# Seven-product steps that add up in place, and one ring for the weight tiles, in a hybrid decoder layer

## The chip, the cores and the metric

The kernel runs on one core of one Trainium2 chip. The metric is the device time of one execution in microseconds; lower is better. Runs of the same kernel agree within about 0.1%.

## What is computed

One inference step of one decoder layer, in float32, on 2048 prompt tokens (one sequence) and 32 sample tokens (eight sequences of four). Cut to what matters here:

```
h = x + mixer(rmsnorm(x))                          # gated linear attention beside a spatial-gating MLP
q = rmsnorm(h) @ wq_x                              # cross attention over 256 memory tokens, 4 heads
p = softmax(q @ mem_k.T / 16)
h = h + (p @ mem_v) @ wo_x
g = rmsnorm(h) @ w_gate                            # 1024 -> 2816
c = conv_b + sum(conv_w[j] * shift(g, j))          # causal depthwise convolution of width 3
h = h + (gelu(c) * (rmsnorm(h) @ w_up)) @ w_down   # 2816 -> 1024
y = rmsnorm(h)
```

It also returns the recurrent and convolution states and the memory keys and values.

## The kernel before

The prompt is worked in four blocks of 512 tokens (`SB`, s = 0 to 3). The 32 sample tokens ride with block 1 in the mixer and with block 2 in the ConvFFN, so block 2's ConvFFN has 544 tokens. Between, during block 1's ConvFFN, the sample tokens' cross attention runs in small steps (`sample_steps`).

*Precision.* Every large product is made of three float32r matmuls (`mm3`): each operand is split into a high part (an ACT copy) and a low part (a DVE subtraction, `split`), and high x high, high x low and low x high are added in PSUM. A float32 weight tile that came by DMA is called raw (tag `wraw`, five buffers); its two parts are `whi` and `wlo` (five buffers each). Weights that were split once can be stored in DRAM and fetched in two parts without a split (`wready`).

*Seven products for eight.* In blocks 1 to 3 the gate and up projections (`gate7`, `upp7`), and in all blocks the scores of the cross attention (`score`), use Strassen's scheme in Winograd's form: the weight matrix and the activations are cut 2 by 2, and seven products of half size take the place of eight. Three products use quarters of the weight matrix as they are (A11, A12, A22, called `PLAIN`), four use sums of quarters (S1 to S4, `SUMS`). `seven_tokens` makes the activations' sums. `seven_make` makes the weights' sums in block 0, from the raw tiles that block 0 needs anyway, and stores them in DRAM: for the gate split in two parts, for up unsplit. A seven-product step (`seven_step`) has seven products of 12 matmuls, each into a PSUM bank or half of one (`acc`, four banks), and combines them with ACT and DVE in a tile q of the raw pool: q0 takes a copy of A11, q3 = S2 + q0, then q1, q2 and q3 get S1 and S3, q0 gets A12, q1 and q2 get S4 and A22. The gate of the first pair in a block (j = 0) runs in an "early" form: all seven banks are open at once, so that most of its work can start before the last activations are there. In block 2 a half has 272 columns, and two halves don't fit a bank; in blocks 1 and 3 it has 256, and two share a bank (`joint`).

*Order.* A list of `Step`s is written out, with side work woven in (`weave`), and `run` goes through it: ahead of each step it issues the loads of later ones, up to `AHEAD` = 5 units further, where a unit is a pair of split tiles (a `seven_tile` counts half). All loads and stores are issued by SP, in one queue. The framework then orders the instructions of each engine when the program is built, by a timeline of its own, from these priorities and from what each instruction waits for, so an instruction may stand ahead of one that comes earlier in the list. On the chip each engine goes through its own order.

*Other tiles.* `U` (49 buffers) and `T_` (6) are general tiles of 544 columns: T holds the gate rows g, the convolved rows c and other short-lived ones.

Of the kernel before, what the change touches and what calls it, by code (L numbers as in the profile page):

```python
# [9 lines left out]
F32 = mybir.dt.float32  # L10
F32R = mybir.dt.float32r
# [18 lines left out]
AHEAD = 5  # L30
NU, NT, NRAW, NW = 49, 6, 5, 5
# [6 lines left out]
def hymba_step_kernel(  # L38
# [16 lines left out]
    wp = ctx.enter_context(tc.tile_pool(name="wp", bufs=NW))  # L55
    npool = ctx.enter_context(tc.tile_pool(name="npool", bufs=8))
# [7 lines left out]
    def T_(name, dt=F32):  # L64
        return tp_.tile([128, TM], dt, tag="T", name=name)
# [25 lines left out]
    def mm3(ps, wh, wl, xh, xl, first, last):  # L91
        pe.matmul(ps, wh, xh, start=first, stop=False)  # L92
        pe.matmul(ps, wh, xl, start=False, stop=False)  # L93
        pe.matmul(ps, wl, xh, start=False, stop=last)  # L94

    def wraw(name):
        return wp.tile([128, 2 * TM], F32, tag="wraw", name=f"r_{name}", bufs=NRAW)

    def wload(w, k0, nk, m0, mw, name):
        raw = wraw(name)  # L100
        r3 = raw[:, :nk * mw].rearrange("p (k m) -> p k m", k=nk)
        nc.sync.dma_start(r3, w[k0 * 128:(k0 + nk) * 128, m0:m0 + mw].rearrange("(k p) m -> p k m", p=128))
        return r3

    def wsplit(raw, name, lo_eng=None):
        sh = list(raw.shape)
        hi = wp.tile(sh, F32R, tag="whi", name=f"h_{name}")
        lo = wp.tile(sh, F32R, tag="wlo", name=f"l_{name}")
        split(hi, lo, raw, lo_eng)
        return hi, lo  # L110

    def wunit(*spec):
        return wsplit(wload(*spec), spec[-1])

    def wraw_unit(*spec):
        return lambda: wload(*spec)

    def wready(src, name):

        def load():  # L120
            out = []
            for x, tag in enumerate(("whi", "wlo")):
                t = wp.tile(list(src.shape[0:1]) + list(src.shape[2:]), F32R, tag=tag, name=f"{tag}_{name}")
# [3 lines left out]
        return load  # L127

    def wkeep(dst, *spec):

        def load():
            out = wunit(*spec)
# [3 lines left out]
        return load  # L136
# [3 lines left out]
    PLAIN, SUMS = ("A11", "A12", "A22"), ("S1", "S3", "S2", "S4")  # L140
    w7n = [0]

    def seven_tile(src, name):

        def load():
            w7n[0] += 1
            t = wp.tile([128, 2, 4, 128], F32R, tag=("whi", "wlo")[w7n[0] % 2], name=name)
            nc.sync.dma_start(t.bitcast(F32), src)
            return t
        load.cost = 0.5  # L150
        return load

    def seven_make(raw, hi, lo, plain, sums, u, name):
# [4 lines left out]
        s13, s24 = U(f"s13{name}"), U(f"s24{name}")  # L158
        h3 = lambda t, i: t[:, i * 256:(i + 1) * 256].rearrange("p (k m) -> p k m", k=2)
        dve.tensor_tensor(h3(s13, 0), a21, a22, ALU.add)  # L160
        dve.tensor_tensor(h3(s13, 1), a11, a21, ALU.subtract)
        dve.tensor_tensor(h3(s24, 0), h3(s13, 0), a11, ALU.subtract)
        dve.tensor_tensor(h3(s24, 1), a12, h3(s24, 0), ALU.subtract)
        ks = slice(2 * u, 2 * u + 2)
        for x, t in enumerate((hi, lo)):
# [4 lines left out]
        for i, t in enumerate((s13, s24)):  # L170
            d = sums[:, 2 * i:2 * i + 2]
            v = lambda t: t.rearrange("p (s k m) -> p s k m", s=2, k=2)
# [33 lines left out]
    def seven_sums(src, name):  # L206

        def load():
            raw = wraw(name)
            nc.sync.dma_start(raw[:, :1024], src.rearrange("p s k m -> p (s k m)"))  # L210
            return wsplit(raw[:, :1024].rearrange("p (k m) -> p k m", k=8), name)
        return load

    def seven_step(plain, sums, get_xs, H, use, name, early=False, then=None):


        seq = ("A11", "S1", "A12", "S2", "S3", "S4", "A22") if early else ("A11", "S2", "S1", "S3", "A12", "S4", "A22")
        joint = 2 * H <= 512 and not early

        units, at = [], {}  # L220
        for nm in seq:
            if nm in PLAIN or len(sums.shape) == 5:
                at[nm] = len(units), None
                units.append(seven_tile(plain[:, PLAIN.index(nm)] if nm in PLAIN else sums[:, SUMS.index(nm)],
                                        f"{name}{nm}"))
            elif nm not in at:
                i = SUMS.index(nm) // 2
                for j in range(2):
                    at[SUMS[2 * i + j]] = len(units), j
                units.append(seven_sums(sums[:, 2 * i:2 * i + 2], f"{name}{nm}"))  # L230

        def fn(*ws):
            def half(nm, x, k):
                u, j = at[nm]
                return ws[u][:, x, k] if j is None else ws[u][x][:, 4 * j + k]

            xs = get_xs()
            last = len(xs) - 1
            q = wraw(f"q_{name}")
            q0, q1, q2, q3 = (q[:, i * H:(i + 1) * H] for i in range(4))  # L240
            ps = {}

            def prod(nm, k0, k1):
                if nm not in ps:
                    mate = {"S3": "S1", "A22": "S4"}.get(nm)
                    if joint and mate:
                        ps[nm] = ps[mate][0], 1
                    else:
                        ps[nm] = (mps if early and len(ps) > 3 else acc)(f"a_{name}{nm}"), 0
                bank, i = ps[nm]  # L250
                for k in range(k0, k1):
                    mm3(bank[:, i * H:(i + 1) * H], half(nm, 0, k), half(nm, 1, k), *xs[k][nm], k == 0, k == last)

            def got(nm):
                return ps[nm][0][:, ps[nm][1] * H:(ps[nm][1] + 1) * H]

            def c11():
                dve.tensor_tensor(q0, got("A12"), q0, ALU.add)

            if early:  # L260
                for nm in seq:
                    prod(nm, 0, last)
            for nm in seq:
                prod(nm, last if early else 0, last + 1)
                if then and nm == "S1":
                    then()
                if nm == "A11":
                    act.activation(q0, got(nm), AF.Copy)
                elif nm == "S2":
# [1573 lines left out]
```

## Time and profile before

| what | value |
|---|---|
| median of three runs | 2832.87 us (2832.57 to 2835.03) |
| the profiled execution | 2837.18 us, of which 2835.5 are the span of the trace |
| TensorE (PE) busy | 2797.1 us, 99% |
| VectorE (DVE) busy | 1894.6 us, 67% |
| ScalarE (ACT) busy | 1106.0 us, 39% |
| GpSimd (POOL) busy | 569.5 us, 20% |
| read from and written to HBM | 507.69 and 127.41 MB |

The ConvFFN of block 0 lies at about 400 to 750 us of the span, block 1's at 1100 to 1500, block 2's at 1820 to 2150, block 3's at 2480 to 2800. In a table by stage, each row begins with the stretch in microseconds; for each engine stands its busy time and the number of its instructions, then the clock that TensorE was granted (1.00 is full), the mean busy share of the sixteen DMA engines, and GB/s. In a time line, a row is start, duration, engine, line, operation and tiles, and in brackets the idle time just before it and what ended that. In a list of groups, the last part is the idle time ahead of the group's instructions and what ended it. PEld is the load of the stationary operand, which overlaps PE.

### The profile page before, as it was taken

The numbers are of one execution on the slowest core, as the hardware profiler recorded it, in microseconds if no ns is written. First come the engines' busy times: TensorE is split into PE (matmuls) and PEld (weight loads), VectorE is DVE, ScalarE is ACT, GpSimd is POOL, SyncE is SP. The second block draws the span as 40 slices with busy tenths as digits, with TensorE's granted clock in tenths as the row PEclk, the third lists the DMA queues.
The fourth block names the chain that finished last, engine by engine and source line by source line (L and its number), as shares of the span: only waits on it lengthen the run. The fifth ranks groups of instructions, "written<-read, shape, count | busy, mean of one in ns | idle before, by whom it ended". The sixth has DMA issues, their size and how long they took to land.

```text
span 2835.5 us, 47052 instructions
## 1 busy us (share of the span) xinstructions
PE 2797.1 (99%) x17894; PEld 2477.9 (87%) x17894; DVE 1894.6 (67%) x3266; ACT 1106.0 (39%) x1950; POOL 569.5 (20%) x638
## 2 busy tenths in 40 slices
PE   8999999999999999999999999999999999999998
PEld 8888888888887898898888889899999888899997
DVE  6578778777657786655555778666666687665555
ACT  5645544333363354223124445422223544431222
POOL 2002213111111221322210121222221022132222
PEclk9999999999999999999999999999999999999999
DMA  9756589999932245888995216577776323677774
GB/s 297 250 182 219 180 267 341 336 343 329 337 112 68 85 154 195 314 288 291 331 324 190 82 60 208 194 252 258 258 269 207 112 69 128 206 260 273 272 281 177
DMA packets 369687, 638.21 MB, mean 225 GB/s; under 512 B 27370, under 2 KB 238412, under 8 KB 369462
## 3 DMA queue, kind: packets, MB, share of 16 engines
q1 hardware_dynamic: 369462, 635.20, 65.7%
q8 instruction: 142, 2.33, 0.3%
q14 instruction: 83, 0.68, 0.1%
HBM read 507.69 MB, written 127.41 MB: 224 GB/s over the span
## 4 chain that ended last, share of the span: by engine, by line
PE 63%; DVE 3%; ACT 1%; issue 0%; POOL 0%; DMA 0%; POOLq 0%; DVEq 0%; ACTq 0%
PE d L94 4%; PE d L92 4%; PE d L93 4%; PE a_wx L94 2%; PE a_wx L93 2%; PE a_wx L92 2%; PE a_wo L92 1%; PE s L1046 1%; PE a_wo L93 1%; PE a_wo L94 1%; PE a_wu L92 1%; PE a_wu L93 1%; PE t_wr L92 1%; PE t_wr L93 1%; PE a_wu L94 1%; PE t_wr L94 1%
## 5 line engine op out<-in xcount | busy, mean ns | idle before, releaser
L92 PE MATMUL d<-acth,whi_wd 128*128 128x272 f32 (+1 forms) x688 | 235.4, 342 | 0.0
L1692 DVE TENSOR_TENSOR h<-d,h 128x512 f32<-128x512 f32 (+1 forms) x232 | 133.7, 582 | 149.4 <-PE d L94 149.2
L94 PE MATMUL d<-acth,wlo_wd 128*128 128x272 f32 (+1 forms) x688 | 233.4, 340 | 0.0
L93 PE MATMUL d<-actl,whi_wd 128*128 128x272 f32 (+1 forms) x688 | 233.3, 339 | 0.0
L1589 POOL TENSOR_TENSOR c<-c,bc_f 128x512 f32<-128x512 f32 (+1 forms) x88 | 137.0, 1562 | 140.4 <-ACT c L1588 139.7
L1579 ACT ACTIVATE c<-g,colsb 128x512 f32<-128x512 f32 x88 | 71.7, 815 | 189.7 <-DVE g L1542 141.7
L94 PEld LDWEIGHTS d<-acth,wlo_wd 128*128 128x128 f32 x688 | 129.5, 188 | 15.5 <-issue 1.2
L93 PEld LDWEIGHTS d<-actl,whi_wd 128*128 128x128 f32 x688 | 129.5, 188 | 13.5 <-issue 0.4
L92 PEld LDWEIGHTS d<-acth,whi_wd 128*128 128x128 f32 x688 | 129.6, 188 | 13.1
L1611 POOL TENSOR_TENSOR c<-r_q_wup,c 128x512 f32<-128x512 f32 (+1 forms) x33 | 63.3, 1918 | 329.4 <-DVE r_q_wup L288 209.6
L92 PE MATMUL a_wo<-ch,h_wo 128*128 128x512 f32 (+1 forms) x320 | 114.3, 369 | 2.0 <-ACT r L876 1.3
L1576 POOL COPY carry<-g 128x2 f32<-128x2 f32 x88 | 29.5, 335 | 420.8 <-DVE g L1542 418.8
L93 PE MATMUL a_wo<-cl,h_wo 128*128 128x512 f32 (+1 forms) x320 | 113.8, 358 | 0.0
L94 PE MATMUL a_wo<-ch,l_wo 128*128 128x512 f32 (+1 forms) x320 | 112.9, 356 | 0.0
L1580 DVE SCALAR_TENSOR_TENSOR c<-g,colsb,c 128x512 f32<-128x512 f32 x88 | 84.9, 965 | 28.3 <-ACT c L1579 27.8
L94 PE MATMUL a_wx<-pTh,wlo_wx 128*128 128x512 f32 x256 | 101.3, 396 | 0.0
L93 PE MATMUL a_wx<-pTl,whi_wx 128*128 128x512 f32 x256 | 100.6, 393 | 0.0
L92 PE MATMUL a_wx<-pTh,whi_wx 128*128 128x512 f32 x256 | 100.2, 394 | 0.0
L84 ACT ACTIVATE acth<-c 128x512 fp32r<-128x512 f32 (+1 forms) x88 | 55.9, 637 | 109.6 <-DVE c L1611 78.0
L1588 ACT ACTIVATE c<-c 128x512 f32<-128x512 f32 (+1 forms) x88 | 56.1, 637 | 94.5 <-DVE c L1581 82.6
L1581 DVE SCALAR_TENSOR_TENSOR c<-g,colsb,c 128x512 f32<-128x512 f32 x88 | 90.6, 1029 | 1.1
L85 DVE TENSOR_TENSOR actl<-c,acth 128x512 fp32r<-128x512 f32 (+1 forms) x88 | 63.1, 720 | 26.6 <-ACT acth L84 25.6
(3753 smaller groups left out, 9741.8 us busy)
## 6 DMA issues: line engine op xcount, KB each, us to landing
whi_wd<-wd SPq DMA_DIRECT2D x66, 512.0 KB, 7.7
wlo_wd<-wd SPq DMA_DIRECT2D x66, 512.0 KB, 7.3
r_wo<-in_w_out_dram SPq DMA_DIRECT2D x32, 512.0 KB, 3.4
wlo_wx<-vod SPq DMA_DIRECT2D x32, 512.0 KB, 4.2
whi_wx<-vod SPq DMA_DIRECT2D x32, 512.0 KB, 5.0
r_wg<-in_w_gate_dram SPq DMA_DIRECT2D x22, 512.0 KB, 7.6
r_wup<-in_w_up_dram SPq DMA_DIRECT2D x22, 512.0 KB, 5.3
r_wd<-in_w_down_dram SPq DMA_DIRECT2D x22, 512.0 KB, 4.5
```

What stands on the lines that cost most here:

```text
L84: act.activation(hi, src, AF.Copy)
L85: (lo_eng or dve).tensor_tensor(lo, src, hi.bitcast(F32), ALU.subtract)
L92: pe.matmul(ps, wh, xh, start=first, stop=False)
L93: pe.matmul(ps, wh, xl, start=False, stop=False)
L94: pe.matmul(ps, wl, xh, start=False, stop=last)
L1579: act.activation(c[:, :SB], g[:, 2:SB + 2], AF.Identity, bias=cb, scale=w2)
L1580: dve.scalar_tensor_tensor(c[:, :SB], g[:, 1:SB + 1], w1, c[:, :SB], ALU.mult, ALU.add)
L1581: dve.scalar_tensor_tensor(c[:, :SB], g[:, 0:SB], w0, c[:, :SB], ALU.mult, ALU.add)
L1588: act.activation(c[:, :T], c[:, :T], AF.Gelu_apprx_tanh)
L1589: pool.tensor_tensor(c[:, :T], c[:, :T], B.fbc[:, :T], ALU.mult)
L1611: (dve, pool)[i].tensor_tensor(c[:, :T], q[i], c[:, :T], ALU.mult)
L1692: dve.tensor_tensor(B.h[m + mm][:, cs], ps[:, :cw], B.h[m + mm][:, cs], ALU.add)
```

## The change

- *One ring.* `whi` and `wlo` become one tag `w` of ten tiles of 1024 columns; `wraw` becomes `raw`, three tiles of 1024 columns. `run` counts, in place of `AHEAD`, which tiles of the ring and which raw tiles (those that a step itself reads) are still to be used, and issues a load when there is room. A seven-product step is seven steps now, one for each product, so a weight tile is given back with its product.
- *In place.* Except in the early gate, the products add up in PSUM along chains: A11, S2, S3 in x; A12 in z; S1, S4 in y; A22 in w. ACT copies x after A11 (to q0) and after S2 (to q1), w after A22 (to q2), y after S1 (to q3); after S3 one DVE operation adds x to q2 and q3, and after S4 one adds z and y to q0 and q1. Where two halves fit a bank, x and w share one, and z and y share one, with y continuing on what z holds. The scores go the same way, with a bank for each chain. The order of the products changes to A11, A12, S2, S1, A22, S3, S4 (scores: A11, S1, A12, S2, A22, S3, S4).
- *Gate sums unsplit.* They are stored like up's: one tile of raw sums for two products, split when it is fetched. The sums are paired S1 with S4 and S2 with S3.
- *Tiles.* q is no raw tile any more: for the gate it is the tile g itself, for up two T tiles. T goes from 6 buffers of 544 columns to 8 of 552, U from 49 to 51.

The diff, cut to its core:

```diff
-AHEAD = 5
-NU, NT, NRAW, NW = 49, 6, 5, 5
+TW = 552
+NU, NT, NW, NR = 51, 8, 10, 3
...
+    def W(name):
+        return wp.tile([128, 1024], F32R, tag="w", name=name)
+    def unit_of(load, ring=2, raws=0, held=False):
+        load.ring, load.raws, load.held, load.until = ring, raws, held, None
+        return load
+    def raw_tile(name):
+        return rp.tile([128, 1024], F32, tag="raw", name=f"w_{name}")
...
-    PLAIN, SUMS = ("A11", "A12", "A22"), ("S1", "S3", "S2", "S4")
+    PLAIN, SUMS = ("A11", "A12", "A22"), ("S1", "S4", "S2", "S3")
+    CHAIN = {"A11": "x", "S2": "x", "S3": "x", "S1": "y", "S4": "y", "A12": "z", "A22": "w"}
+    COPIED = {"A11": 0, "S2": 1, "A22": 2, "S1": 3}
...
     # seven_make
-            if len(sums.shape) == 4:
-                nc.sync.dma_start(d[:, :, ks], v(t[:, :512]))
-                continue
-            sh, sl = U(f"sh{i}{name}", F32R), U(f"sl{i}{name}", F32R)
-            split(sh[:, :512], sl[:, :512], t[:, :512])
-            for x, o in enumerate((sh, sl)):
-                nc.sync.dma_start(d[:, :, x, ks], v(o[:, :512].bitcast(F32)))
+            nc.sync.dma_start(sums[:, 2 * i:2 * i + 2, ks], t[:, :512].rearrange("p (s k m) -> p s k m", s=2, k=2))
...
     # seven_step, one product
+        def part(nm, *ws):
+            i = CHAIN[nm]
+            if nm in loads:
+                hold(nm, *ws)
+            if nm == "A11":
+                st.q, st.at = outs(), {}
+            if i not in st.at:
+                if joint:
+                    t = acc(f"a_{name}{i}")
+                    for n, o in enumerate("xw" if i in "xw" else "zy"):
+                        st.at[o] = t[:, n * H:(n + 1) * H]
+                    if i in "zy":
+                        st.zy = t[:, 0:2 * H]
+                else:
+                    st.at[i] = acc(f"a_{name}{i}")[:, :H]
+            fresh = nm in ("A11", "A12") or not joint and nm in ("S1", "A22")
+            for k in range(last + 1):
+                mm(st.at[i], nm, k, fresh and k == 0, k == last)
...
+            if nm in COPIED:
+                act.activation(quarters(q)[COPIED[nm]], st.at[i], AF.Copy)
+            elif nm == "A12" and not joint:
+                q0 = quarters(q)[0]
+                dve.tensor_tensor(q0, st.at["z"], q0, ALU.add)
+            elif nm == "S3":
+                q23 = q[1].rearrange("p (s t) -> p s t", s=2)
+                dve.tensor_tensor(q23, st.at["x"].unsqueeze(1).broadcast_to([128, 2, H]), q23, ALU.add)
+            elif nm == "S4":
+                if joint:
+                    dve.tensor_tensor(q[0], st.zy, q[0], ALU.add)
...
+        parts = {nm: Step(lambda *ws, nm=nm: part(nm, *ws), [unit(nm)] if nm in loads else []) for nm in seq}
+        for nm in SUMS[::2]:
+            parts[nm].units[0].until = parts[SUMS[SUMS.index(nm) + 1]]
+        return Step(None, parts=list(parts.values()))
...
     # run
-            need += sum(cost(u) for u in st.units)
-            while at < len(queue) and made < need + AHEAD:
+            for live in (ring, raws):
+                while live and live[0][1] < i:
+                    live.pop(0)
+            while at < len(queue):
                 j, u = queue[at]
...
+                if not (room(ring, "ring", u.ring, NW) and room(raws, "raws", u.raws, NR)):
+                    break
...
     # score
-        SEQ = ("A11", "S1", "A12", "S2", "S3", "S4", "A22")
+        SEQ = ("A11", "S1", "A12", "S2", "A22", "S3", "S4")
...
+                fresh = nm in ("A11", "S1", "A12", "A22")
+                if fresh:
+                    B.ps[CHAIN[nm]] = acc(f"sc{s}{i}{nm}")
+                ps = B.ps[CHAIN[nm]]
...
+                if nm in COPIED:
+                    o = COPIED[nm]
+                    q[o] = T_(f"p{s}{i}{o}")
+                    act.activation(q[o][:, :512], ps, AF.Copy)
+                for o in {"A12": (0,), "S3": (3, 2), "S4": (1,)}.get(nm, ()):
+                    dve.tensor_tensor(q[o][:, :512], ps, q[o][:, :512], ALU.add)
+                    soften(i, o)
```

More of the change, by code (lines that the diff above doesn't have):

```diff
@@ L485, in run, with room @@
     def run(steps):
+        steps = [p for st in steps for p in st.parts]
+        index = {st: i for i, st in enumerate(steps)}
         queue = [(i, u) for i, st in enumerate(steps) for u in st.units]
-        cost = lambda u: getattr(u, "cost", 1)
         ready = {}
-        made = need = 0
+        ring, raws = [], []
+        made = {"ring": 0, "raws": 0}
         at = 0
+        def room(live, kind, n, size):
+            return not live or made[kind] + n - live[0][0] <= size
         for i, st in enumerate(steps):
@@ L742, in load @@
                 return raw, *wsplit(raw, f"{name}{j}")
-            return load
-        return [Step(lambda wu, j=j: fn(j, wu), [unit(j)]) for j in range(4)]
+            return unit_of(load, 2, 1, sample)
+        out = [Step(lambda wu, j=j: fn(j, wu), [unit(j)]) for j in range(4)]
+        for j in (0, 2) if sample else ():
+            out[j].units[0].until = out[j + 1]
+        return out
     def norm_in_steps(B):
```

290 lines of the change are left out of this document (125 added, 165 removed).

## The prediction

> **What bounds the kernel now.** I read the page's busy times first, then the busy time by stage, then what each engine waited for, and last the time line around the places that the change touches.
>
> ```profile
> span 2835.5 us, 47052 instructions
> PE 2797.1 (99%) x17894; PEld 2477.9 (87%) x17894; DVE 1894.6 (67%) x3266; ACT 1106.0 (39%) x1950; POOL 569.5 (20%) x638
> HBM read 507.69 MB, written 127.41 MB: 224 GB/s over the span
> ```
>
> ```profile
> core 0: us, PE busy (x) PEld busy (x) DVE busy (x) ACT busy (x) POOL busy (x), PEclk, DMA share, GB/s
> 0.00:50.00 50.00, 41.21 (x301) 38.90 (x302) 31.48 (x62) 30.27 (x58) 14.85 (x57) 1.00 0.93 297
> 400.00:750.00 350.00, 350.00 (x1525) 285.13 (x1525) 269.54 (x430) 142.40 (x188) 66.88 (x72) 1.00 1.04 332
> 1010.00:1038.00 28.00, 24.24 (x185) 23.06 (x183) 27.92 (x55) 19.68 (x35) 11.56 (x8) 0.99 0.28 84
> 1038.00:1050.00 12.00, 11.88 (x76) 11.56 (x76) 5.78 (x12) 2.90 (x5) 2.66 (x3) 0.74 0.30 101
> 1050.00:1500.00 450.00, 450.00 (x3322) 400.45 (x3321) 256.40 (x401) 133.69 (x229) 106.20 (x121) 1.00 0.82 294
> 1850.00:2150.00 300.00, 300.00 (x2397) 300.00 (x2397) 192.01 (x347) 73.26 (x117) 78.81 (x119) 1.00 0.74 262
> 2500.00:2800.00 300.00, 300.00 (x2138) 281.21 (x2137) 175.51 (x247) 71.08 (x105) 80.11 (x82) 1.00 0.78 276
> ```
>
> TensorE bounds it. In the four ConvFFN stages (the 400, 1050, 1850 and 2500 rows) PE is busy for every microsecond while DVE, ACT and the DMA engines have room, except in block 0, where the DMA share is 1.04 and PE is full all the same. PE loses time in few places: 8.8 us in the first 50, and 3.8 us in 1010 to 1038, where DVE is busy for 27.92 of 28 us and the clock then drops to 0.74 for 12 us (another 3.1 us). Over the whole span PE is idle for 2835.5 - 2797.1 = 38 us, so no edit that leaves the matmuls alone can win much more than 1.5%.
>
> **The change, part by part.** The matmuls stay: 66 seven-product steps of 84 and 56 score products of 24, with the same shapes. Thus the sum is made of PE's waits alone.
>
> *Sums in place.* Before, each product had a bank or half of one, and DVE combined them; now A11, S2 and S3 add up in x, S1 and S4 in y, and ACT copies A11, S2, A22 and S1 out in between.
>
> ```profile
> L275 DVE TENSOR_TENSOR r_q_wg<-a_wg13S,r_q_wg x1: 692/692/692, 1231.3 to 1231.3; 128x512 f32<-128x512 f32 x1
> L281 DVE TENSOR_TENSOR r_q_wg<-a_wg13S,r_q_wg x1: 424/424/424, 1232.0 to 1232.0; 128x256 f32<-128x256 f32 x1
> L84 ACT ACTIVATE sh0wg<-s13wg 128x512 fp32r<-128x512 f32 x22 | 13.9, 633 | 46.9 <-DVE s13wg L161 45.5 <-DMA wd<-l_wd 1.3
> L85 DVE TENSOR_TENSOR sl0wg<-s13wg,sh0wg 128x512 fp32r<-128x512 f32 x22 | 15.0, 682 | 0.0
> L84 ACT ACTIVATE h_wup<-r_wup 128x1024 fp32r<-128x1024 f32 x22 | 23.3, 1057 | 26.9 <-PE d L93 15.4 <-issue 3.6 <-PE a_wg L93 3.4
> L85 DVE TENSOR_TENSOR l_wup<-r_wup,h_wup 128x1024 fp32r<-128x1024 f32 x22 | 28.1, 1279 | 6.1 <-ACT h_wup L84 6.0
> ```
>
> DVE: a step with both halves in one bank (42 of them: blocks 1 and 3 without the early gate) goes from 3 x 0.42 + 2 x 0.69 = 2.6 us to 2 x 0.69 = 1.4; the 21 of block 2 from seven operations to three, about -1.4 each; the eight score groups lose three of 0.69. Together -53 - 29 - 17 = -99 us. *Gate sums unsplit:* 66 splits are added where the gates run, 66 x 1.28 = +84 us on DVE and 66 x 1.06 = +70 on ACT; 44 half-size ones go from block 0, -30 and -28. DVE ends about 45 us lower, ACT with 189 copies of 0.38 (row below) and 24 in the scores of about 0.6 some 128 us higher, at 44% of the span. Both lie beside a full PE: DVE has 125 us free in the 300 of the last stage, ACT 229, so neither total reaches the end: 0. The sums' DMAs halve for the gates: 33 steps x 1 MB less read, 11 MB less written, and SP issues 66 loads and 44 stores fewer. Block 0 is relieved, but PE was full there: 0. If that cover went, its bound is the DMA share of 1.04, and it falls.
>
> *What is new on the path* is that PE now waits for ACT. S2 may not start before A11 is copied, with one product (A12) between; A22 and S3 sit likewise behind copies. Before, the A11 copy (L268) had nobody waiting, so its lateness is ACT's own queue, and it can be read off:
>
> ```profile
> 2614.82 0.28 PE L94 MATMUL a_wup34A<-w1wx,wup34A 128*128 128x256 f32 x1
> 2614.94 0.28 PE L92 MATMUL a_wup34S<-wuhwx,h_wup34S 128*128 128x256 f32 x1
> 2615.14 0.38 ACT L268 ACTIVATE r_q_wup<-a_wup34A 128x256 f32<-128x256 f32 x1 [11.60 <-PE a_wup34A L94]
> ```
>
> ```profile
> L94 PE MATMUL a_wg11A<-w1wx,wg11A x4: 280/282/284, 1149.8 to 1150.9; 128*128 128x256 f32 x4
> L94 PE MATMUL a_wg19A<-w1wx,wg19A x4: 274/280/282, 1439.1 to 1440.1; 128*128 128x256 f32 x4
> L94 PE MATMUL a_wg110A<-w1wx,wg110A x4: 275/280/283, 1462.4 to 1463.5; 128*128 128x256 f32 x4
> ```
>
> ```profile
> 1154.69 0.63 ACT L84 ACTIVATE acth<-c 128x512 fp32r<-128x512 f32 x1 [0.51 <-POOL c L1611]
> 1155.22 0.36 ACT L268 ACTIVATE r_q_wg<-a_wg11A 128x256 f32<-128x256 f32 x1
> 1440.11 0.63 ACT L760 ACTIVATE junk<-x 128x512 bf16<-128x512 f32 x1 [11.71 <-DMA x<-in_x_prompt_dram]
> 1444.19 0.36 ACT L268 ACTIVATE r_q_wg<-a_wg19A 128x256 f32<-128x256 f32 x1
> 1467.46 0.38 ACT L268 ACTIVATE r_q_wg<-a_wg110A 128x256 f32<-128x256 f32 x1 [1.97 <-PE sop L1406]
> 1840.37 0.38 ACT L268 ACTIVATE r_q_wg<-a_wg21A 128x272 f32<-128x272 f32 x1
> 2503.26 0.36 ACT L268 ACTIVATE r_q_wg<-a_wg31A 128x256 f32<-128x256 f32 x1
> ```
>
> The usual case is the first: the matmul that starts last at 2614.82 has its copy done at 2615.52, 0.70 us later. The next products follow at 0.12 us a matmul, so with A12's twelve between, S2 could start 0.12 + 12 x 0.12 = 1.55 us after: covered. Of the 63 copies of steps that will chain, the rows show three in block 1 that came late, because ACT, in order, stood behind something else: an activation split behind POOL, a square that waited 11.71 us for the DMA of x, a sample matmul. Their lateness over 1.55 us: 1155.58 - 1150.9 - 1.55 = 3.1; 1444.55 - 1440.1 - 1.55 = 2.9; 1467.84 - 1463.5 - 1.55 = 2.8. Two more, the second gates of blocks 2 and 3 (1840.37, 2503.26), end about 2.1 us after their last matmul: 0.5 each. Sum 9.8 us. Bounds: 0, if the order of the engines, which is planned anew, puts other matmuls there; and twice 9.8 if S2's copies, with the same cover, meet as much. I take one draw, since a stop of 3 us at A11 has let the blocking instruction pass before S2 is done, and leave out the case that hangs on the DMA of x, as the sums that crowd its queue are halved: **+7 us**.
>
> *Order of the scores.* S3 moves behind A22, so of the first five units fetched ahead only S1 and S2 need a split.
>
> ```profile
> L85 DVE TENSOR_TENSOR l_qk10S<-r_qk10S,h_qk10S 128x1024 fp32r<-128x1024 f32 x3 | 3.7, 1218 | 0.0
> 1034.85 1.21 DVE L85 TENSOR_TENSOR l_qk10S<-r_qk10S,h_qk10S 128x1024 fp32r<-128x1024 f32 x1
> ```
>
> The third split, at 1034.85, lies inside the stretch where DVE holds PE up; moved on, it gives back its 1.2 us. Bounds: 0, and all of 3.8 + 3.1 = 6.9 with the clock. I take the nearest row: **-1.2 us**.
>
> *One ring of ten, three raw tiles.* Ten split tiles were there before (two tags of five); released product by product they hold the same number in flight. Raw tiles fall from five to three.
>
> ```profile
> 3.40 5.19 SPq L102 DMA_DIRECT2D r_wk<-in_wk_x_dram  x5
> 18.13 0.38 SPq L102 DMA_DIRECT2D r_wk<-in_wk_x_dram  x1
> 25.08 1.06 ACT L84 ACTIVATE h_wk<-r_wk 128x1024 fp32r<-128x1024 f32 x1 [4.35 <-DMA r_wk<-in_wk_x_dram]
> r_wd<-in_w_down_dram SPq DMA_DIRECT2D x21, 512.0 KB, 4.5
> r_wup<-in_w_up_dram SPq DMA_DIRECT2D x20, 512.0 KB, 5.3
> r_wg<-in_w_gate_dram SPq DMA_DIRECT2D x19, 512.0 KB, 8.2
> ```
>
> In block 0 a raw tile lives for a transfer (4.5 to 8.2 us) plus the split (1.06 + 1.28), 7 to 11 us; three of them deliver a unit each 2.3 to 3.5 us, while PE takes 24 x 0.23 = 5.5 us for one (350 us / 1525 matmuls): covered. SP's order changes with it: what stands behind a load that waits for a raw tile are the stores of the split weights, and their cover is the four units held ahead. At the start there is no cover: five loads go out at once, the sixth at 18.13, and ACT then waits 4.35 us for it. With three, the fourth and fifth must wait for the first split (DVE ends it about 12.2 us), 7 us later than now, but the sixth no longer stands behind the loads of x. Bounds: -2.7 and +4; I take **+1.5**.
>
> *T 6 to 8, U 49 to 51.* The q tiles leave the raw pool for T (two per step), so T's room is as before; no wait of the rows above names a U tile: 0.
>
> Sum: 7 - 1.2 + 1.5 = +7.3 us. The profiled execution took 2837.18 us for its span of 2835.5, 1.7 around it; the median of the runs shown is 2832.87, 4.3 under. On the median: 2832.87 + 7.3 = **2840**.
>
> **The rivals.**
> *A: it stays hidden.* 58 of the 63 copies were in time, and the order is planned with the new waits in it, so PE may be given `d`, next-step or sample matmuls to run meanwhile. For: PE full in all three stages. Against: ACT's late ones come from waits of up to 11.7 us. Then only the small terms are left: 2833.
>
> *B: faster.* DVE loses the third split and PE's pause at 1028 to 1038 closes. It decides once DVE is about 4 us ahead in that stretch, for then the clock does not drop either: -6.9, with the start's 1.5 won as lost, 2825. Against: nothing else of DVE's 27.92 us there goes away.
>
> *C: halves of a bank wait for each other.* In 42 steps x and w lie in one bank, and S3 stands right behind A22. If a matmul into one half is held until the copy of the other is done, each such step stops for 0.70 - 0.12 = 0.58 us: 42 x 0.58 = 24 us, 2857. For: the order written out has nothing in between. Against: S4 writes the other bank and could be put there.
> The Trainium skill, "PSUM — Partial Sum Buffer", section "PSUM bank collisions raise a hardware error", says that engines must be kept apart by bank and quadrant, not by address; by it the copy of A22 and S3 cannot overlap, and the sum would be C's unless other matmuls fill in. The trace of before has no matmul into a bank with a reader at work in its other half, so it does not show this.
>
> **How the numbers follow.** Forecast 0.38, A 0.30, B 0.20, C 0.12. About 0.2% (5.7 us) is what a measurement here can tell from no change; a tenth of the forecast's chance falls below it. Slower 0.34 + 0.12 = 0.46, same 0.30 + 0.04 = 0.34, faster 0.20. The range reaches from B's 2825 to C with some of the forecast's term, 2861; the forecast alone holds 2835 to 2852 (0 to 20 for the late copies).
>
> **What would show it.** Chain waits: PE idle in front of a_wg or a_wup with an ACT copy as releaser, most of it in block 1 (1100 to 1500), PE no longer 450 of 450. C: the same pause of about 0.6 us in every step of block 3. Scores: two splits instead of three in the stretch before the scores of block 1, and PE's loss there under 3.8. Start: PE under 41.2 of the first 50. The forecast is wrong if PE stays full in the ConvFFN stages, or if a whole stage starves for weights because three raw tiles are too few, which no term above prices.

## The result, and the profile after

The changed kernel took 2880.33 us (median of six runs, 2875.52 to 2883.46), the kernel before 2834.95 beside it (2832.57 to 2839.88): a ratio of 1.0158, with an interval from 1.0144 to 1.0172. It is some 45 us slower, outside the range of the prediction (2825 to 2861 around 2840). The profiled execution took 2877.25 us, 40 more than that of before. Runs of the kernel before, beside all the kernels below, lie between 2830.6 and 2841.5 us but for one of 9728, so they agree within 0.4%, not the 0.1% given at the top.

The page after, its head and its line of HBM traffic:

```profile
span 2875.5 us, 46693 instructions
PE 2807.7 (98%) x17894; PEld 2482.3 (86%) x17894; DVE 1835.4 (64%) x3054; ACT 1216.2 (42%) x2185; POOL 562.7 (20%) x638
HBM read 473.09 MB, written 115.87 MB: 205 GB/s over the span
```

The volumes moved much as forecast: DVE by -59 (forecast -45), ACT by +110 (forecast +128), HBM by -34.6 and -11.5 MB. The time went the other way, because PE is idle for 2875.5 - 2807.7 = 68 us instead of 38, and it is busy 10.6 us longer for the same matmuls. The granted clock, 0.995 of full over the span before and 0.992 after, makes some 8 to 9 us of that by an estimate from the two; what makes the rest isn't shown. The busy times by stage (the start, then the four ConvFFN stages), and after them the two stages of the kernel before that lost most, over the same work:

```profile
0.00:50.00 50.00, 41.35 (x301) 38.61 (x301) 30.72 (x61) 29.17 (x59) 13.73 (x57) 1.00 0.88 274
424.00:774.00 350.00, 350.00 (x1540) 285.27 (x1539) 242.68 (x391) 120.16 (x156) 53.42 (x69) 1.00 0.99 318
1136.00:1547.00 411.00, 400.96 (x2979) 354.55 (x2978) 226.11 (x291) 150.06 (x259) 98.99 (x116) 0.99 0.75 261
1838.00:2209.00 371.00, 370.58 (x2962) 369.95 (x2961) 227.35 (x391) 147.17 (x262) 102.86 (x140) 1.00 0.62 220
2503.00:2865.00 362.00, 352.68 (x2442) 326.37 (x2442) 193.52 (x252) 130.43 (x220) 78.12 (x93) 0.99 0.62 214
```

```profile
1126.00:1524.00 398.00, 398.00 (x2978) 352.77 (x2977) 225.76 (x333) 110.71 (x176) 99.11 (x116) 1.00 0.83 297
2479.00:2825.00 346.00, 346.00 (x2442) 322.76 (x2441) 201.02 (x295) 87.17 (x137) 86.85 (x93) 1.00 0.71 254
```

Blocks 1 and 3, where two sums of a gate or up step share a bank, have the same 2979 (one more than before, at the edge of the stretch) and 2442 matmuls in 411 and 362 us that took 398 and 346. Block 2, with a bank for each sum, is full. Some of what PE waited for in the kernel after: a wait in block 1's mixer (t_wr1q), and the longest ones ahead of gate and up products, of which the kernel before had none over 0.2 us (total, times, longest):

```profile
PE t_wr1q L745 <- DMA w_wr<-in_w_in_dram: 4.0, 1, 4.0
PE a_wup15x L93 <- ACT q L292: 2.6, 1, 2.6
PE a_wg32x L93 <- DMA wg32A<-w7g: 2.5, 1, 2.5
PE a_wg16x L93 <- DMA wg16A<-w7g: 2.3, 1, 2.3
PE a_wg12x L93 <- DVE c L1605: 2.2, 1, 2.2
PE a_wg38x L93 <- DMA wg38A<-w7g: 2.1, 1, 2.1
PE a_wg310x L93 <- DVE nct L1780: 1.6, 1, 1.6
PE a_wg18x L93 <- DMA wg18A<-w7g: 1.4, 1, 1.4
PE a_wg34x L93 <- DMA wg34A<-w7g: 1.2, 1, 1.2
```

Only one of these ends on a copy by ACT. The others of the ConvFFN stages stand before A11 of an even gate, the first of a group, and most end on the load of its weight tile. How block 3 gets there shows in PE's order, taken from the time line as products (start in us; a product that is split stands once, where it begins):

```
before  2500.15 wg31: A11 S2 S1 S3 A12 S4 A22   2510.05 wup31: A11 S2 S1 S3 A12 S4 A22   2519.95 wg32: A11
after   2526.04 wup30 S4, S3 | 2528.89 wg31 S2, S4 | 2531.72 wup31 A11, A12 | 2533.70 wg31 A22
        2536.07 wup31 S1 | 2537.48 wg31 S3 | pause | 2541.65 wg32 A11, A12, S1 | 2547.53 wup31 S2
```

The list has A22, S3, S4 at the end of a step; the order that was planned has the next step's A11, A12 and S1 in between, since A22 goes into the half bank beside x and must wait for the copy of S2, and S3 for the copy of A22. Two steps thus want weight tiles at once: up to 14 by count (three single tiles and two pairs for each), and the ring has ten. The load of wg32's tile goes out late, behind SP's other waits. The first row below shows why: ACT's split of wup31's sums had to wait until 2528.73 for a tile of the ring that a product of wup30 still read. The raw tile of these sums came free only after the split, at 2532, and SP stood for it with the loads of wg32 behind it (ACT, SP, then PE, from the time line):

```profile
2528.73 2.01 ACT L85 ACTIVATE h_wup31S<-w_wup31S 128x1024 fp32r<-128x1024 f32 x2 [1.29 <-PE a_wup30x L95]
```

```profile
2528.60 0.32 SPq L154 DMA_DIRECT2D wup31A<-w7u  x1
2532.03 0.32 SPq L206 DMA_DIRECT2D w_wg32S<-s7g  x1
2532.41 0.42 SPq L154 DMA_DIRECT2D wup31A<-w7u  x1
2533.77 0.32 SPq L206 DMA_DIRECT2D w_wup32S<-s7u  x1
2534.18 1.44 SPq L154 DMA_DIRECT2D wg32A<-w7g  x2
```

```profile
2538.90 0.27 PE L1778 MATMUL ncp<-ident,carry 128*2 128x128 f32 x1
2541.65 0.36 PE L93 MATMUL a_wg32x<-w1wx,wg32A 128*128 128x256 f32 x1 [2.48 <-DMA wg32A<-w7g]
```

### The profile page after: what moved, and what is told of

The parts are those of the page before. It is cut to its first block, busy times and chain, and to the rows that moved or that the text cites. A ratio compares the mean times of both kernels' runs of the same rounds, so it can differ in the third digit from the quotient of the medians.

```text
span 2875.5 us, 46693 instructions
## 1 busy us (share of the span) xinstructions
PE 2807.7 (98%) x17894; PEld 2482.3 (86%) x17894; DVE 1835.4 (64%) x3054; ACT 1216.2 (42%) x2185; POOL 562.7 (20%) x638
## 4 chain that ended last, share of the span: by engine, by line
PE 83%; DMA 6%; DVE 5%; ACT 3%; issue 2%; POOL 1%; SPq 0%; POOLq 0%; ACTq 0%; DVEq 0%
PE d L95 6%; PE d L93 6%; PE d L94 6%; PE a_wx L95 2%; PE a_wx L94 2%; PE a_wx L93 2%; PE s L1082 2%; PE a_wg L95 1%; PE a_wup L95 1%; PE a_wup L93 1%; PE a_wg L93 1%; PE a_wg L94 1%; PE a_wup L94 1%; PE a_wu L95 1%; PE a_wu L93 1%
## 5 line engine op out<-in xcount | busy, mean ns | idle before, releaser
L93 PE MATMUL d<-acth,h_wd 128*128 128x512 f32 (+1 forms) x864 | 305.0, 354 | 0.9 <-DMA h_wd<-wd 0.9
L95 PE MATMUL d<-acth,l_wd 128*128 128x512 f32 (+1 forms) x864 | 302.6, 351 | 1.3 <-DMA l_wd<-wd 1.3
L94 PE MATMUL d<-actl,h_wd 128*128 128x512 f32 (+1 forms) x864 | 303.2, 351 | 0.0
L95 PEld LDWEIGHTS d<-acth,l_wd 128*128 128x128 f32 x864 | 162.4, 188 | 24.1 <-DMA l_wd<-wd 2.1
L93 PEld LDWEIGHTS d<-acth,h_wd 128*128 128x128 f32 x864 | 162.4, 188 | 22.7 <-PE sop L1429 1.4
L94 PEld LDWEIGHTS d<-actl,h_wd 128*128 128x128 f32 x864 | 162.7, 188 | 20.5 <-issue 0.6
L1636 POOL TENSOR_TENSOR c<-q,c 128x512 f32<-128x512 f32 (+1 forms) x33 | 48.5, 1470 | 412.7 <-DVE q L298 289.5
L95 PE MATMUL a_wx<-pTh,l_wx 128*128 128x512 f32 x256 | 100.7, 394 | 0.0
L94 PE MATMUL a_wx<-pTl,h_wx 128*128 128x512 f32 x256 | 100.3, 393 | 0.0
L93 PE MATMUL a_wx<-pTh,h_wx 128*128 128x512 f32 x256 | 98.8, 394 | 0.0
L1605 DVE SCALAR_TENSOR_TENSOR c<-g,colsb,c 128x512 f32<-128x512 f32 x88 | 69.6, 795 | 16.3 <-ACT c L1604 16.3
```

Of the source, the lines that this page charges most:

```text
L93: pe.matmul(ps, wh, xh, start=first, stop=False, skip_group_check=again)
L94: pe.matmul(ps, wh, xl, start=False, stop=False, skip_group_check=again)
L95: pe.matmul(ps, wl, xh, start=False, stop=last, skip_group_check=again)
L1605: dve.scalar_tensor_tensor(c[:, :SB], g[:, 1:SB + 1], w1, c[:, :SB], ALU.mult, ALU.add)
```

## The experiments

Beside the kernel after, fourteen kernels were run. For each the table has the median, its ratio to the kernel before with the interval, and, from the profiled executions, how much longer than before each stretch took (us; from the first matmul of one tile to that of the next). A stretch "to FFN n" is block n's mixer and scores; the first begins at the program's start. Each stretch comes from one execution; in the last row, where nothing changed in the median, stretches still differ by up to 2.4 us.

| kernel | median us | ratio | to FFN 0 | FFN 0 | to FFN 1 | FFN 1 | to FFN 2 | FFN 2 | to FFN 3 | FFN 3 |
|---|---|---|---|---|---|---|---|---|---|---|
| after | 2880.3 | 1.0158 [1.0144, 1.0172] | +7.4 | -0.1 | +2.3 | +13.1 | +0.8 | +0.3 | +0.2 | +16.0 |
| four banks | 2867.5 | 1.0116 [1.0097, 1.0135] | +9.3 | -0.1 | +4.8 | +12.0 | +0.9 | +1.2 | -0.5 | +3.1 |
| four banks, 49 U | 2862.6 | 1.0092 [1.0073, 1.0112] | +7.9 | -2.7 | +5.6 | +6.8 | +3.4 | +0.7 | -0.6 | +3.8 |
| four raw tiles | 2859.7 | 1.0078 [1.0062, 1.0095] | -1.3 | -0.9 | -3.2 | +10.0 | +3.7 | +1.5 | -0.7 | +13.0 |
| four banks, four raw | 2842.5 | 1.0026 [1.0017, 1.0036] | +2.1 | -0.9 | -1.8 | +3.1 | +1.8 | +0.1 | +0.3 | +1.1 |
| ring of eleven | 2873.9 | 1.0134 [1.0120, 1.0148] | +12.6 | +1.6 | +1.9 | +10.2 | -0.1 | +1.4 | -1.4 | +6.9 |
| control 48 U, 7 T | 2905.8 | 1.0247 [1.0232, 1.0262] | +16.2 | +3.8 | +7.7 | +16.3 | +2.2 | +1.9 | +1.4 | +14.4 |
| ring of twelve, 48, 7 | 2885.5 | 1.0177 [1.0162, 1.0192] | +20.3 | +3.2 | +5.4 | +9.3 | +2.2 | +4.6 | +1.6 | +4.1 |
| five raw, 48, 7 | 2874.1 | 1.0135 [1.0120, 1.0150] | -3.5 | +4.9 | +3.6 | +17.1 | +1.4 | +0.2 | +0.3 | +13.0 |
| S4 first | 2884.5 | 1.0170 [1.0151, 1.0189] | +7.9 | -0.1 | +4.7 | +12.7 | +1.4 | +0.5 | +0.1 | +17.7 |
| products apart | 2865.3 | 1.0110 [1.0091, 1.0129] | +6.1 | -0.1 | +4.8 | +9.7 | +1.4 | +0.1 | +0.6 | +4.7 |
| apart, four raw | 2848.3 | 1.0046 [1.0031, 1.0060] | -1.8 | -0.9 | -1.7 | +8.0 | +1.1 | +0.3 | -0.3 | +4.1 |
| copies by DVE | 2854.0 | 1.0062 [1.0047, 1.0077] | -3.1 | -0.9 | -2.0 | +5.4 | +1.2 | +5.5 | -0.2 | +8.7 |
| S1 first | 2847.7 | 1.0041 [1.0027, 1.0054] | +0.4 | -0.9 | -1.8 | +8.5 | +0.7 | +1.9 | +0.5 | +3.6 |
| before, gate sums unsplit | 2835.2 | 0.9996 [0.9987, 1.0006] | +0.2 | -2.3 | +1.5 | -2.4 | +1.0 | +0.1 | -1.0 | +1.6 |

**Four banks for four sums.**

```
-        joint = 2 * H <= 512
+        joint = False
```

> Blocks 1 and 3 take their four gate sums in four banks, as block 2 does, instead of two sums to a bank. Nothing else is edited: same ring of ten, same three raw tiles, same list of products. The kernel after stands at 2880; its two feed-forward stages with two sums to a bank lost 13.1 and 16.0 us against the kernel before, block 2's with a bank for each sum 0.3. Theory 1 (two sums in one bank make S3 wait for the copy of A22, the planned order puts S4 and the next step's A11, A12 and S2 ahead of it, two steps hold their weight tiles at once and the next A11 is loaded late): both stages come back to within 3 us of the kernel before, the order of the products is the list's, the pauses of 2 to 3 us at the even gates are gone; 2851 to 2856. Theory 2 (ten tiles given out product by product are too few whatever the banks are): the pauses at even gates stay, 2875 to 2883. Theory 3 (the copies of ScalarE come late and hold TensorE): 2875 to 2883 too, with pauses that end on a ScalarE copy.

Half of theory 1 held. Block 3's FFN came back to +3.1, but block 1's stayed at +12.0. In block 3 PE's order is nearly the list's again (wup31 runs A11, A12, S1, A22, S2, S4 before wg32's A11; only its S3 comes after), and the stage is full:

```profile
2506.00:2856.00 350.00, 349.01 (x2447) 323.87 (x2445) 201.06 (x274) 129.12 (x221) 90.55 (x94) 1.00 0.63 221
```

So block 1 has a second cause. In this run it is mostly what theory 3 had, though in one place only: PE waits 4.6 us at wup15 for a copy by ACT, and the clock stands at 0.50 for the 6.8 us behind it, another 3.4 us, together 8 of the 12.

```profile
PE a_wup15x L93 <- ACT q L292: 4.6, 1, 4.6
1340.50:1347.30 6.80, 5.54 (x26) 5.54 (x27) 1.27 (x4) 2.13 (x7) 0.00 (x0) 0.50 0.17 60
```

**S4 ahead of S3 in the list**, two sums to a bank:

```
-("A11", "A12", "S2", "S1", "A22", "S3", "S4")
+("A11", "A12", "S2", "S1", "A22", "S4", "S3")    # blocks 1 and 3
```

> Blocks 1 and 3 keep two sums to a bank, but the list has S4 ahead of S3, so that S3, which waits for the copy of A22, has S4's 12 products before it. Theory 1: the planned order no longer pulls the next step's products forward, the weight tiles are given back as in the list, 20 to 29 us of the 29 come back: 2851 to 2860. Theory 2 (ten tiles too few): no change, 2875 to 2883. Theory 3 (late copies): between them, since S3 gets 3 us more for its copy, 2865 to 2878 with pauses still ended by ScalarE.

A miss: 2884.5, and block 3 at +17.7. The planned order mixed the steps no less: wup31's S2 and S4 and its A22 stood behind wg32's A11, as before. Moving S4 in the list didn't undo the overlap; taking away the shared banks, in the run above, did.

**A longer ring**, first of twelve, with a control that has its small tiles alone, then of eleven:

```
-NU, NT, NW, NR = 51, 8, 10, 3
+NU, NT, NW, NR = 48, 7, 12, 3    # ring of twelve
+NU, NT, NW, NR = 48, 7, 10, 3    # control
+NU, NT, NW, NR = 49, 8, 11, 3    # ring of eleven
```

> Twelve tiles in the ring instead of ten; to make room, 48 and 7 of the other two kinds of tile instead of 51 and 8. Banks and order of the list are as in the kernel after. Two steps that overlap want 14 tiles by the trace. Theories 1 and 2: the load of the next A11 goes out one product earlier (about 1.4 us, and a landing of some 6 us was late by 2.5), so the pauses at even gates shrink from 2.5 to about 1 us or go: feed-forward stages of blocks 1 and 3 gain 15 to 29 us, 2851 to 2866. Theory 3 (late copies of ScalarE): no gain, 2875 to 2885. The start of blocks 0 and 1 (some 10 us lost there) isn't touched by any theory except that of the three raw tiles, which says it stays.

> Control for the two runs that took 48 and 7 of the small tiles to make room (ring of twelve, five raw tiles): here only these two numbers are changed, ring of ten and three raw tiles as in the kernel after. Those two runs lost 3 to 5 us more in block 0's feed-forward stage, and the ring of twelve lost 17 us in block 0's mixer where the five raw tiles gained 2. If the fewer small tiles are the price: block 0's mixer about +17 us and its feed-forward stage +3 to +5 us against the kernel before, 2888 to 2900. If the ring of twelve and the five raw tiles bring these losses themselves: as the kernel after, 2878 to 2884.

> The kernel after with eleven tiles in the ring instead of ten (49 instead of 51 of one kind of small tile makes room, which by itself gave 0 to 5 us with four banks); two sums to a bank and three raw tiles as in the kernel after. Between the control with 48 and 7 small tiles and the ring of twelve beside it, block 3's feed-forward stage gained 10 us, block 1's 7. If the overlap of two steps costs because the ring is too short for it: block 3's feed-forward stage loses 8 to 12 us against the kernel before instead of 16, the pauses at its even gates shrink, 2866 to 2875 in all. If the length of the ring isn't it: block 3's stays at 15 to 17, 2875 to 2881.

By itself the ring of twelve looked useless (2885.5). The control shows why: three U and one T fewer cost 25 us (2880.3 to 2905.8), more than the expectation had put on it. Against its control the ring of twelve gains 20 us, of which 10.3 in block 3's FFN and 7.0 in block 1's. The ring of eleven, which needs only two U tiles, takes block 3's FFN from +16.0 to +6.9 with the banks still shared; in that block its pauses at the even gates are 0.4 to 1.0 us, where the longest were 1.2 to 2.5:

```profile
PE a_wg32z L93 <- DMA wg32A<-w7g: 1.0, 1, 1.0
PE a_wg310x L93 <- DMA wg310A<-w7g: 0.6, 1, 0.6
PE a_wg36x L93 <- DMA wg36A<-w7g: 0.4, 1, 0.4
PE a_wg34x L93 <- DMA wg34A<-w7g: 0.4, 1, 0.4
PE a_wg38x L93 <- DMA wg38A<-w7g: 0.4, 1, 0.4
```

So shared banks cost through the tiles that two overlapping steps hold: either giving each sum its bank or lengthening the ring takes most of block 3's loss away. The ring of eleven also has two U tiles fewer, and no control for that was run with shared banks; with four banks these two made no difference to block 3's FFN (+3.1 and +3.8).

**More raw tiles.**

```
-NU, NT, NW, NR = 51, 8, 10, 3
+NU, NT, NW, NR = 48, 7, 10, 5    # five raw tiles
+NU, NT, NW, NR = 49, 8, 10, 4    # four raw tiles; also with joint = False
+NU, NT, NW, NR = 49, 8, 10, 3    # control for the latter, with joint = False
```

> Five raw tiles instead of three; 48 and 7 of the other two kinds of tile instead of 51 and 8, ring of ten. Theory 4 (three raw tiles are too few where every unit comes raw, in the loads and folding of blocks 0 and 1): the stretches up to block 0's scores and up to block 1's scores, which lost 7.3 and 4.7 us, come back to within 2 us each, 2868 to 2871; the two feed-forward stages stay as they are (29 us lost). Rival (these stretches lose for the order in which the loads are issued, or for the ring shared by split halves and gate tiles): no change, 2877 to 2883. If three raw tiles are what starves the feed-forward stages too, these gain as well: 2840 to 2855.

> Four banks for four sums in blocks 1 and 3, and four raw tiles (49 instead of 51 of one kind of small tile makes room). Four banks alone measured 2867.5: block 3's feed-forward stage came back (+3 us against the kernel before), block 1's did not (+12). Five raw tiles brought back 11 us in block 0's mixer and none in block 1's. Theory: the two gains lie in different stages and add; four raw tiles give between half and all of the 11: 2857 to 2863, with block 1's feed-forward stage still +12. Rival (each frees the other's next wait, or four are as short as three): 2864 to 2870.

> Two sums in a bank as in the kernel after, with four raw tiles (49 instead of 51 of one kind of small tile): the fourth corner beside the kernel after (2880), four banks (2867.5), and four banks with four raw tiles (2842.5). If the two causes add: 2880 less 25, so 2851 to 2859, with block 3's feed-forward stage still +13 to +16 us and block 1's between +4 and +8. If the fourth raw tile only helps where each sum has its bank: 2866 to 2880.

> Control for the run with four banks and four raw tiles: four banks, three raw tiles, 49 instead of 51 of one kind of small tile. If the fourth raw tile made the 25 us, nothing comes of this: 2866 to 2873. If it was another order of the loads and steps that came with the other tile count: 2842 to 2855.

With four banks and 49 U, the fourth raw tile gains 20.1 us (2862.6 to 2842.5). With shared banks it gains 20.6 (2880.3 to 2859.7), and here the two U tiles fewer are part of the edit: with four banks they alone gained 4.9 us. The banks gain 12.8 us with three raw tiles (2880.3 to 2867.5) and 17.2 with four (2859.7 to 2842.5). So the two gains add, within some 5 us. Against its control, the run with five raw tiles gains 31.6 us, 19.7 of them before FFN 0; by itself, at 2874.1, it had fallen between its two expectations.

Three expectations missed in part. Four banks and four raw tiles came out on the good side: block 1's FFN was left at +12 and stands at +3.1. Most of this isn't the raw tile's: the control with 49 U alone has +6.8, with a pause at wup15 of 2.0 us instead of 4.6 and no low clock behind it. Four raw tiles with shared banks has block 1's FFN at +10.0, where 4 to 8 was expected. The control itself, 2862.6, lies under the 2866 to 2873 that was to show that the two U tiles do nothing.

Before FFN 0, where the kernel after loses 7.4 us, PE is idle for 20.4 us; it was 14.8 before and is 15.1 with four raw tiles and shared banks. Two waits, new in the kernel after, go with the fourth raw tile: colpsb's falls to 0.5 us and qkp's to none. PE reads raw tiles here too, in the fold of wq, and SP stands behind it (PE, then SP, in the kernel after):

```profile
PE colpsb L411 <- DMA rowsb<-in_g_sgu_dram: 2.5, 1, 2.5
PE qkp L93 <- ACT wqh L85: 1.7, 1, 1.7
SPq L109 <- PE wqp L636: 3.8, 1, 3.8
```

Which of SP's waits makes which of PE's isn't shown there; in block 1's mixer it is. In the kernel after, SP waited 35.0 us at one stretch in this mixer. In block 1's FFN it waited, with loads of gate and up sums (L206), behind a matmul of the sampled tokens; no pause of PE is shown to come from that (total, times, longest):

```profile
SPq L109 <- PE t_wr1q L745: 40.0, 2, 35.0
SPq L206 <- PE sqp L1429: 19.2, 3, 10.9
```

```profile
960.90 1.07 PE L745 MATMUL t_wr1q<-w_wr,sxg 128*32 128x512 f32 x8
965.94 1.93 PE L745 MATMUL t_wr1q<-w_wr,sxg 128*32 128x512 f32 x8 [3.98 <-DMA w_wr<-in_w_in_dram]
962.02 0.38 SPq L109 DMA_DIRECT2D w_wr<-in_w_in_dram  x1
```

These units are read raw by PE, and a tile is kept from its load until PE's order reaches them: SP stood 35 us for one, issued the next load at 962.02, and PE waited 3.98 us for it. With four raw tiles and four banks, SP still waits there (37.2 us), but the next tile is already loaded, PE no longer waits there, and no load of sums (L206) stands behind sqp.

**The products apart**, as in the kernel before, on the new ring (here the part of the loop that differs):

```
-seq = ... ("A11", "A12", "S2", "S1", "A22", "S3", "S4")
+seq = ... ("A11", "S2", "S1", "S3", "A12", "S4", "A22")
+bank, n = (st.at[mate][0], 1) if joint and mate else (acc(f"a_{name}{nm}"), 0)   # mates: S1 S3, S4 A22
+if nm == "A11": act.activation(q0, got(nm), AF.Copy)
+elif nm == "S2": dve.tensor_tensor(q3, got(nm), q0, ALU.add)
...
```

> The new ring with its ten tiles and three raw ones, given back product by product, and the gate sums kept unsplit, but the seven products go apart into banks and are combined by VectorE as in the kernel before (in its order A11, S2, S1, S3, A12, S4, A22, with S1 and S3, and S4 and A22, in one bank in blocks 1 and 3); one copy by ScalarE a step instead of four, and no product waits for a copy. VectorE's work goes back up, by some 50 to 100 us in all. Theory (the chains that add up in place are what costs: through the planned order in block 3, through TensorE's waiting for ScalarE in block 1): both feed-forward stages come within 4 us of the kernel before, 2850 to 2860; what stays is block 0's and block 1's mixer (+7 and +2 to +5). Rival (ten tiles given out product by product are too few): both stay at +10 or more, 2870 to 2884.

> The products apart as in the run beside it, and four raw tiles (49 instead of 51 of one kind of small tile). If the chains and the three raw tiles are the two causes and nothing else costs: 2838 to 2850, block 0's mixer within 3 us of the kernel before. If the ring is short by itself: 2864 to 2880.

With three raw tiles 2865.3, a little over the expected 2860, with block 3 at +4.7 and block 1 at +9.7, where 4 at most was expected for each; with four, 2848.3, within what was expected. Without the chains block 3's FFN thus loses some 4 us, not 16. Block 1's loses 8, and that isn't the ring's alone: in both runs PE waits 3.1 us at wup15, here too for a copy by ACT (that of A11, L289), so the expectation's "no product waits for a copy" doesn't hold.

```profile
PE a_wup15S L93 <- ACT q L289: 3.1, 1, 3.1
```

Adding up in place, with a bank for each sum, is 5.8 us faster than this with four raw tiles (2842.5 against 2848.3), and about the same with three (2867.5 and 2865.3).

**The copies by DVE**, on four banks and four raw tiles:

```
-act.activation(quarters(q)[COPIED[nm]], st.at[i], AF.Copy)
+dve.tensor_copy(quarters(q)[COPIED[nm]], st.at[i])
```

> Four banks and four raw tiles (2842.5), and the four copies of a step are made by VectorE instead of ScalarE (168 copies; VectorE has 35% of its time free, ScalarE's copies took 0.38 us each). Theory (ScalarE's order holds the copies: its exponential of the sampled attention waits for VectorE and loads a table, and a copy for TensorE stands behind it): the pause of 1.9 us at block 1's a_wup15x goes, with the low clock behind it, 2836 to 2841. Rival (VectorE's own queue holds the copies longer than ScalarE's): 2844 to 2860.

**S1 ahead of S2**, on the same kernel: `("A11", "A12", "S1", "S2", "A22", "S4", "S3")`.

> Four banks and four raw tiles (2842.5), and the list is A11, A12, S1, S2, A22, S4, S3: each product that waits for a ScalarE copy has two products ahead of it (2.8 us) instead of one, but for S3, which has A22 and S4 either way. If the rest of the loss is the short cover of the copies: the pause at a_wup15x goes and block 1's feed-forward stage comes within 1 us of the kernel before, 2835 to 2840. If the rest lies elsewhere: 2841 to 2845. If the pair of S1 and S4, now loaded a product earlier and held over S2, starves the ring: 2846 to 2860.

Both are slower than what they were built on (2854.0 and 2847.7 against 2842.5). With DVE's copies the pause at wup15 stays, now behind DVE, and blocks 2 and 3 lose 5 and 8 us more, as the rival had it. With S1 first it grows, to 4.3 us with 3.4 us of low clock behind it, which make most of block 1's +8.5; the number lies in the range for a starved ring, but PE's longest wait for a weight there is 1.1 us. The pause with four banks and four raw tiles, with DVE's copies, and with S1 first, then ACT's time line of the last:

```profile
PE a_wup15x L93 <- ACT q L292: 1.9, 1, 1.9
```

```profile
PE a_wup15x L93 <- DVE q L292: 2.5, 1, 2.5
```

```profile
PE a_wup15x L93 <- ACT q L292: 4.3, 1, 4.3
```

```profile
1317.91 0.63 ACT L1614 ACTIVATE c<-c 128x512 f32<-128x512 f32 x1 [2.24 <-DVE c L1607]
1319.67 1.28 ACT L1501 ACT_TABLE_LOAD   x1 [1.13 <-DVE smx L1500]
1320.97 0.56 ACT L1501 ACTIVATE sp<-ssc,smx,srp 128x256 f32<-128x256 f32 x1
1321.43 0.19 ACT L1501 ACTIVATION_READ_ACCUMULATOR sp<-ssc,smx,srp 128x1 f32 x1
1321.53 0.37 ACT L292 ACTIVATE q<-a_wup15x 128x256 f32<-128x256 f32 x1
```

The copy of wup15's A11 stands in ACT's order behind the exponential of the sampled attention, which waits for DVE's maximum and loads a table first. A longer cover in the list doesn't move it forward: what counts is what the copy is queued behind.

**The kernel before with the gate sums unsplit:**

```
-[128, 4, 2, 4, 128] if nm == "g" else [128, 4, 4, 128]
+[128, 4, 4, 128]
```

> The kernel before with one part of the change: the gate sums are stored unsplit, as those of up are, and split again for each gate product pair. The prediction put this part at nothing. If so: 2830 to 2839. If the additional splits (2 a gate, each some 1 us on ScalarE and 1 us on VectorE) or the raw tiles that they take hold TensorE: 2840 to 2855. If the 34.6 MB less read help: 2820 to 2829.

No difference: 2835.16, a ratio of 0.9996 from 0.9987 to 1.0006.

## Why the prediction was wrong, point by point

- **"One ring of ten, three raw tiles: covered"** failed, and weighed most: some 20 of the 45 us. The working took a raw tile's life as transfer plus split, 7 to 11 us, and asked whether block 0's ConvFFN is fed; that stage did stay full (350 of 350). But units that PE reads raw, in the fold of wq, in block 1's mixer and in its sampled attention, keep their tile until PE gets to them. SP stood 35 us for such a tile in one case, and nothing in the sum priced that. The start, the only place priced, showed 41.35 of the first 50 us busy where a loss was forecast, though block 0's first product came 2 us later. The prediction had named the starving of a whole stage as what would make it wrong; it was several stretches instead.
- **"Released product by product they hold the same number in flight"** failed for blocks 1 and 3: 13 to 17 us (2880.3 to 2867.5 with three raw tiles, 2859.7 to 2842.5 with four, where only the banks differ). The count of tiles is the same, but the step of the sum took PE's order to be the list's. The waits for copies in a shared bank made the planned order overlap two steps, which want 14.
- **Rival C** (2857) had the place, blocks 1 and 3, and the direction, at a chance of 0.12. Its price came from a pause of 0.58 us in each of 42 steps; that pause never occurred. Of the 252 copies of these sums in the trace after, none ran while a matmul wrote to the same tile of PSUM, and but for one pause, at wup15, the order filled the waits with other products. The bill came as late weights before the even gates. The Trainium skill, "PSUM — Partial Sum Buffer", section "PSUM bank collisions raise a hardware error", has engines kept apart by bank and quadrant, not by address. These copies and matmuls were kept apart by bank; what a collision would do no run here shows.
- **Chain waits, +7.** The term was real but is not where it was put. None of the three copies that came late before (wg11, wg19, wg110) stopped PE. One did, at wup15: 2.6 us, and 1.7 more by the half clock of the 3.4 us behind it. It stands in every version with the copies, at 1.4 to 4.6 us, since this copy is queued behind the exponential of the sampled attention, which the term didn't have. With the two causes above removed, 7.5 us remain (2842.5 against 2835). 3.1 of them lie in block 1's FFN, and this pause (1.9) with its low clock (1.7 again) makes these. What makes the other 4 or so wasn't settled.
- **Gate sums unsplit, 0:** right, by the run that made this edit alone.
- **Order of the scores, -1.2:** not shown by itself, as no run makes this edit alone. PE's waits ahead of block 1's scores, 3.8 us before, are 2.9 in the kernel after, 3.6 with four raw tiles and 2.3 with four banks and four raw tiles: the sign fits, and the size lies among them.
- **"T 6 to 8, U 49 to 51: 0"** can't be judged for itself, but the sizes aren't free: 48 and 7 cost 25 us, while 49 with four banks gained 5.

No version of the changed kernel run here beat the kernel before. The nearest is four banks and four raw tiles, 0.26% slower.

## What to carry to other kernels

A tile's life is not transfer plus use: it lasts until the engine's order reaches its last reader. So when a pool is cut, look in the profile for the loader's own waits (which row of SP ends on which matmul) in every stretch that draws on that pool. A new dependency between engines can cost nothing where it lies and yet reorder the work around it; ask which buffers are then held at once, before asking how long the wait is. When room for an experiment is taken from another pool, run that pool's cut alone beside it: here the ring of twelve seemed useless until its control had run.

## What the runs showed of the hardware

A pause of PE can cost more than its length. After the 2.5 us at wg32 matmuls took 0.415 us instead of 0.28, while after the 1.2 us at wg34 they kept their pace. The rows show the second product after each pause (minimum, median, maximum in ns), and then the stretch after wg32's pause, with the clock at 0.50:

```profile
L93 PE MATMUL a_wg32z<-wbhwx,wg32A x4: 415/416/416, 2543.4 to 2545.4; 128*128 128x256 f32 x4
L93 PE MATMUL a_wg34z<-wbhwx,wg34A x4: 277/280/283, 2611.8 to 2612.9; 128*128 128x256 f32 x4
2542.80:2546.20 3.40, 3.40 (x18) 3.40 (x17) 2.43 (x3) 1.30 (x4) 0.13 (x2) 0.50 0.17 51
```

The low clock lasted some 3.4 us. The length of the pause alone doesn't decide it: in the kernel after, 2.1 us at wg38, 2.2 at wg12 and 2.6 at wup15 were followed by it too, 2.3 at wg16 was not. The Trainium skill, "TensorE: Matmul & The Clock Gate", section "Part 1: The HAM clock gate (the "warmup" mystery)", puts the fall to half rate after an idle window of about 3.4 us; here 2.1 to 2.6 us of idle were enough in four cases of five, and the measurement decides.

A load's issue can be far from its use: wg32's first two tiles were issued at 2534.18 and 2535.31, and PE was released at 2541.65, 6 to 7.5 us later. That is more than four products of 1.4 us each (12 matmuls at 0.12). The DMA engines were busy for 0.90 of that time, though only for 0.62 of the whole stage.
